# Attention's values as one product of blocks: seven block products in place of eight

## The chip, the cores and the metric

The kernel runs on one core of one Trainium2 chip. The core has five engines that run their own instruction streams and wait for each other on semaphores: TensorE (PE in the profile; its weight loads are PEld), VectorE (DVE), ScalarE (ACT), GpSimd (POOL), and SyncE (SP), which here issues nearly all of the loads. The metric is the device time of one execution in microseconds. The kernel before takes 977.26 us, the median of three runs (977.25 to 977.32). A difference of under 0.2% (about 2 us) can't be told from no change here.

## What is computed

Two layers on 512 frames of 1024 channels, all in float32. Layer 0 mixes frames by pooling, layer 1 by attention; each is followed by a gated MLP with a short convolution. The change is in layer 1, in the product that makes the attention's values. Cut to that part:

```python
h = rmsnorm(x, mix_norm[1])            # 512 frames x 1024 channels
qkv = h @ w_qkv                        # 1024 -> 3 * 1024
q, k, v = jnp.split(qkv, 3, axis=-1)
q = head_rmsnorm(q.reshape(B, S, N_HEADS, HEAD_DIM), q_norm)
k = head_rmsnorm(k.reshape(B, S, N_HEADS, HEAD_DIM), k_norm)
v = v.reshape(B, S, N_HEADS, HEAD_DIM)
...
p = jax.nn.softmax(s, axis=-1).astype(vb.dtype)
return jnp.einsum('bhqk,bkhd->bqhd', p, vb)
```

The values are thus the product of a 512 x 1024 matrix of frames and a 1024 x 1024 matrix of weights.

## The kernel before, in words

The residual stream lies in eight tiles `X[k]` of 128 channels x 512 frames. A product in full precision is made of three fast products: every operand is split into a high part (a rounded copy, made by ScalarE) and a low part (the rest, made by a subtraction on VectorE), and `mm3` (L117) sends three matmuls to TensorE: high x high, high x low, low x high (L119, L120, L121). `split` (L93) makes the two parts (L98 on ScalarE, L99 on VectorE), `split_scaled` (L101) the same with a factor per partition (L103, L104), and `load_split` (L106) loads a tile of weights of 128 x 1024 into one of three raw buffers (DMA at L113) and splits it into one of two pairs of buffers, `wh` and `wl`.

`ffn` (L377) is the gated MLP. Most of its hidden tiles are made by `strassen` (L532), which already spends seven block products where eight would be plain; the differences of its weight blocks are VectorE's (L537 to L540). Its last group of output products (`out`, adds to `X` at L608) is the work just ahead of the attention.

`attention` (L641) first makes `XS`, the scaled stream split in high and low parts (16 tiles, in `set2`). Then, in this order of the code: `project(0)` (L671), the queries and keys of the first four heads; `late`, which holds the squares of these, their sums (L681) and the norms made from them (L697); `values(0)` and `values(1)` (L707), the two halves of 512 value channels; between these `channel_major` (L750) twice, the transposes of the first heads' queries and keys (L756). Each of `project` and `values` goes through `products` (L658): four weight tiles of 128 x 1024 (two groups of 128 input channels each), and for each group four tiles of 128 frames, so 8 x 4 x 3 = 96 matmuls of 512 columns into four PSUM banks. A half's four results are divided among the tiles `set1`, as `V`, by 16 calls of `split_scaled` on 128 x 128 pieces, with the factor `rcol` of each frame.

Then comes the loop over 16 heads and four tiles of 128 frames (`scores`, `turn`, `mix`: scores, their transposes, the mix of the values), with the rest of the projections and the output product as fill. `scores` reads the bias of its head from one of two tiles `BT`, which SyncE loads from memory (L781). Before the first scores, 44 matmuls of `project(1)` run as fill; its weights' low parts are made by GpSimd, not by VectorE.

What sets the order: in the loop over the heads and in `ffn`, TensorE's order is written out by hand (`manual_schedule`). The part that the change touches, `project(0)` to `values(1)`, has no order written out for any engine: a planner in the framework orders each engine's instructions when the kernel is built. The memory comes from pools with a lifetime: `ffn(0)` has the pool `b0`, the attention `ba` in the same place after it, the second `ffn` `b1`. PSUM has eight banks, under three names: four called S, two P, two Q.

Of the kernel before, what the change touches and what calls it, by code (L numbers as in the profile page):

```python
# [68 lines left out]
def trunk(ctx: ExitStack, tc: tile.TileContext, xt, xT, cols, band, edge, poolw, gv, wout, wqk, wv, wo, rel, out):  # L69
# [15 lines left out]
    def psum(tag, name, bufs=2):  # L85
        return ps.tile([P, S], F32, name=name, tag=tag, bufs=bufs)
# [6 lines left out]
    def split(raw, hi, lo, eng=None, eng_hi=None):  # L93

        if eng_hi:
            eng_hi.tensor_copy(hi, raw)
        else:
            nc.scalar.activation(hi, raw, AF.Copy)  # L98
        return (eng or nc.vector).tensor_sub(lo, raw, hi.bitcast(F32))  # L99
# [17 lines left out]
    def mm3(o, sh, sl, mh, ml, first, last):  # L117

        yield nc.tensor.matmul(o, sh, mh, start=first, stop=False)  # L119
        yield nc.tensor.matmul(o, sh, ml, start=False, stop=False)  # L120
        yield nc.tensor.matmul(o, sl, mh, start=False, stop=last)  # L121

    def run(steps):
        step = None
        for step in steps:
            pass
        return step
# [513 lines left out]
    def attention():  # L641
# [2 lines left out]
        O2 = {}  # L644


        PT = [[big.tile([P, 4 * (TT - 1) + 1, P], F32R, name=f"pt{b}{c}") for c in "hl"] for b in range(2)]

        KL = [[big.tile([P, S], F32R, name=f"kl{b}{e}") for e in range(2)] for b in range(2)]
        for b in range(2):  # L650
            for e in range(2):
                nc.gpsimd.memset(KL[b][e][(1 - e) * HD:(2 - e) * HD].bitcast(F32), 0.0)
        BT = [big.tile([P, S], F32, name=f"B{b}") for b in range(2)]
        for b in range(2):
            nc.gpsimd.memset(BT[b][:HD, :HD], -NEG)
        V = {}

        def products(ov, w, name, eng=None, evict=None):  # L658

            for kk in range(4):  # L660
                hi, lo = load_split(w[kk], 1024, f"{name}_{kk}", eng=eng)

                for c, t in [(c, t) for c in range(2) for t in range(TT)] if kk < 3 else [(c, t) for t in range(TT) for c in range(2)]:
                    k = 2 * kk + c
                    s = slice(c * S, (c + 1) * S)
                    q = slice(t * P, (t + 1) * P)
                    yield from mm3(ov[t], XS[k][:, q], XS[KD + k][:, q], hi[:, s], lo[:, s], k == 0, k == KD - 1)
                    if kk == 3 and c and evict:
                        evict(t)
# [34 lines left out]

            late.append(norms)

        def values(half, banks):  # L707
            ov = [psum(banks[t // 2], f"v{half}_{t}", BANKS[banks]) for t in range(TT)]

            def evict(t):  # L710
                for hh in range(2):
                    V[t, 2 * half + hh] = vt = set1[(t * 2 + half) * 2 + hh].rearrange("p (h a d) -> p h a d", h=4, a=2)
                    v4 = ov[t][:, hh * 256:(hh + 1) * 256].rearrange("p (h d) -> p h d", d=HD)
# [4 lines left out]
            yield from products(ov, wv[half], f"wv{half}", evict=evict)  # L718

        def output(ps_, after=None):  # L720

# [51 lines left out]
        def scores(h, t):  # L773

            p, e = divmod(h, 2)
            q, k, kl = QK[p, 0][e], QK[p, 1][e], KL[p % 2][e]
            if t == 0:

                base = rdram[h, :]
                for r, n in ((0, S - HD), (HD, S)):  # L780
                    nc.sync.dma_start(BT[h % 2][r:r + HD, S - n:], bass.AP(tensor=base.tensor, offset=base.offset + HD, ap=[[1, HD], [1, n]]))  # L781
            n = (t + 1) * P
            nw = max(n, 256)

            sc = psum("S", f"sc{h}_{t}", 4)
            nc.tensor.matmul(sc[:, :nw], q[:, t * P:n], k[:, :nw], start=True, stop=False)
            nc.tensor.matmul(sc[:, :nw], q[:, t * P:n], kl[:, :nw], start=False, stop=True)
            SM[h, t] = s_ = big.tile([P, n], F32, name=f"sb{h}_{t}", tag=f"sb{t}")
# [16 lines left out]
        def mix(h):  # L805

            p, e = divmod(h, 2)
            hs = slice(e * HD, (e + 1) * HD)
            oo = psum("S", f"oo{h}", 4)
            if p not in O2:  # L810
                O2[p] = big.tile([P, S], F32, name=f"o2_{p}", tag="o2", bufs=4)
# [25 lines left out]
        with tc.manual_schedule(engines={mybir.EngineType.PE}):  # L837
# [37 lines left out]
                    kept += 1  # L875
            fill(nb + FO)
        assert kept == NPAIR
        return lambda after: output((6, 7), after)

    def last_pairs(rest, c, name):  # L880
# [90 lines left out]
```

## Time and profile before

| what | value |
|---|---|
| median of three runs | 977.26 us |
| span of the profiled execution | 975.1 us |
| left around the span, against the median | 2.16 us |
| TensorE busy | 967.0 us (99%) |
| VectorE busy | 807.8 us (83%) |
| ScalarE busy | 541.4 us (56%) |
| GpSimd busy | 103.2 us (11%) |
| granted TensorE clock | 1.000 |

The profiled execution's time is its span and what lies around it; the profile states the span alone, so 2.16 us is taken as constant. The attention's part that matters here goes from 380 us, where the last output product of the first `ffn` ends, to 454.7 us, where the first scores start. The profile is read in stages: the whole-run shares in the table say which engine is busiest on average, and a row over a stretch says which one is short of time there. A row of the timeline gives the start, the duration, the engine, the line, the operation, and in brackets the idle time before it and what ended that.

### The profile page before, as it was taken

The page shows a single profiled execution, that of the slowest core. Times are in us where ns is not written, and L with a number is a line of the kernel's source. Part 1 is how long each engine was busy: PE and PEld are TensorE (multiplying, and loading weights), DVE is VectorE, ACT ScalarE, POOL GpSimd, SP SyncE. Part 2 cuts the span into 40 slices and gives each one's busy share as a digit, 9 for nine tenths or more (in the row PEclk, how much of TensorE's full clock was granted, in tenths as well). Part 3 has the DMA queues.
Part 4 walks back from the last instruction along what each step waited for, and adds up shares of the span by engine and source line. Part 5 has one row for each costly group of instructions (what it writes and reads, how often), then busy time and mean ns, then how long its engine had stood idle before and what let it go on. Part 6 is the DMA issues. An engine that isn't in the chain of part 4 may idle for free.

```text
span 975.1 us, 15058 instructions
## 1 busy us (share of the span) xinstructions
PE 967.0 (99%) x5582; PEld 847.0 (87%) x5582; DVE 807.8 (83%) x1468; ACT 541.4 (56%) x926; POOL 103.2 (11%) x90
## 2 busy tenths in 40 slices
PE   9999999999999999999999999999999999999998
PEld 8788999998899888888888787888999989899986
DVE  8999989999999854442777887999989998999953
ACT  7665454544454544345898988656545444455421
POOL 2300000000000013204534442000000000000000
PEclk9999999999999999999999999999999999999999
DMA  9222323333333234232333341232333333233323
GB/s 341 70 85 71 117 89 111 119 113 98 104 92 103 68 90 150 89 119 96 112 114 105 96 118 54 87 110 79 104 110 118 92 105 111 86 117 98 100 71 111
DMA packets 37433, 102.91 MB, mean 106 GB/s; under 512 B 4432, under 2 KB 7904, under 8 KB 37360
## 3 DMA queue, kind: packets, MB, share of 16 engines
q1 hardware_dynamic: 37296, 101.90, 33.7%
q8 instruction: 44, 0.72, 0.3%
q14 instruction: 29, 0.24, 0.1%
q0 software_dynamic: 32, 0.04, 0.0%
q10 hardware_dynamic: 32, 0.00, 0.0%
HBM read 95.60 MB, written 2.14 MB: 100 GB/s over the span
## 4 chain that ended last, share of the span: by engine, by line
PE 94%; DVE 4%; ACT 2%; issue 0%; DMA 0%; DVEq 0%; ACTq 0%
PE out L120 8%; PE out L119 8%; PE out L121 8%; PE st_t L120 5%; PE st_t L119 5%; PE st_t L121 5%; PE st_b L120 4%; PE st_b L119 4%; PE st_b L121 4%; PE st_t L555 4%; PE gv L120 4%; PE gv L119 4%; PE gv L121 4%; PE qk L120 3%; PE qk L119 3%; PE qk L121 3%
## 5 line engine op out<-in xcount | busy, mean ns | idle before, releaser
L98 ACT ACTIVATE g_h<-gv_r 128x1024 fp32r<-128x1024 f32 x68 | 57.7, 848 | 79.2 <-PE st_t L120 37.5
L120 PE MATMUL out<-one,ow_h 128*128 128x512 f32 x224 | 88.1, 393 | 0.0
L119 PE MATMUL out<-one,ow_h 128*128 128x512 f32 x224 | 87.8, 392 | 0.0
L121 PE MATMUL out<-one,ow_l 128*128 128x512 f32 x224 | 87.7, 392 | 0.0
L98 ACT ACTIVATE ow_h<-wo_r 128x640 fp32r<-128x640 f32 (+1 forms) x64 | 50.5, 789 | 59.6 <-PE out L120 47.0
L608 DVE TENSOR_TENSOR X<-out,X 128x512 f32<-128x512 f32 (+1 forms) x65 | 43.9, 677 | 38.1 <-PE out L121 37.8
L98 ACT ACTIVATE g_h<-sa 128x1024 fp32r<-128x1024 f32 x34 | 36.1, 1060 | 59.1 <-PE st_t L120 42.4
L99 DVE TENSOR_TENSOR g_l<-gv_r,g_h 128x1024 fp32r<-128x1024 f32 x68 | 64.6, 950 | 4.8 <-ACT g_h L98 4.5
L99 DVE TENSOR_TENSOR ow_l<-wo_r,ow_h 128x640 fp32r<-128x640 f32 (+1 forms) x64 | 56.5, 882 | 0.0
L419 DVE SCALAR_TENSOR_TENSOR c<-a,col,c 128x511 f32<-128x511 f32 (+1 forms) x76 | 56.2, 742 | 0.1
L120 PE MATMUL st_t<-h,g_h 128*128 128x256 f32 x192 | 54.3, 283 | 0.0
L119 PE MATMUL st_t<-h,g_h 128*128 128x256 f32 x192 | 54.3, 283 | 0.0
L121 PE MATMUL st_t<-h,g_l 128*128 128x256 f32 x192 | 54.3, 283 | 0.0
L121 PE MATMUL st_t<-two,g_l 128*128 128x256 f32 x192 | 54.0, 281 | 0.0
L120 PE MATMUL st_t<-two,g_h 128*128 128x256 f32 x192 | 53.9, 281 | 0.0
L119 PE MATMUL st_t<-two,g_h 128*128 128x256 f32 x192 | 53.8, 280 | 0.0
L121 PE MATMUL qk<-wqk_h,two 128*128 128x512 f32 x128 | 51.4, 402 | 0.0
L119 PE MATMUL qk<-wqk_h,two 128*128 128x512 f32 x128 | 50.8, 409 | 0.0
L120 PE MATMUL qk<-wqk_l,two 128*128 128x512 f32 x128 | 50.8, 397 | 0.0
L121 PEld LDWEIGHTS out<-one,ow_l 128*128 128x128 f32 x224 | 42.3, 189 | 6.6
L119 PEld LDWEIGHTS out<-one,ow_h 128*128 128x128 f32 x224 | 42.4, 189 | 5.9
L120 PEld LDWEIGHTS out<-one,ow_h 128*128 128x128 f32 x224 | 42.5, 190 | 5.3 <-DVE one L99 0.2
(331 smaller groups left out, 3154.3 us busy)
## 6 DMA issues: line engine op xcount, KB each, us to landing
gv_r<-gv SPq DMA_DIRECT2D x86, 512.0 KB, 3.6
wo_r<-wout SPq DMA_DIRECT2D x32, 384.0 KB, 3.1
wo_r<-wout SPq DMA_DIRECT2D x32, 320.0 KB, 2.9
wqk_r<-wqk SPq DMA_DIRECT2D x16, 512.0 KB, 3.5
wv_r<-wv SPq DMA_DIRECT2D x8, 512.0 KB, 3.5
wo_r<-wo SPq DMA_DIRECT2D x8, 512.0 KB, 3.5
xt<-xt SPq DMA_DIRECT2D x4, 512.0 KB, 5.2
X<-xT SPq DMA_DIRECT2D x8, 256.0 KB, 7.5
```

What stands on the lines that cost most here:

```text
L98: nc.scalar.activation(hi, raw, AF.Copy)
L99: return (eng or nc.vector).tensor_sub(lo, raw, hi.bitcast(F32))
L119: yield nc.tensor.matmul(o, sh, mh, start=first, stop=False)
L120: yield nc.tensor.matmul(o, sh, ml, start=False, stop=False)
L121: yield nc.tensor.matmul(o, sl, mh, start=False, stop=last)
L419: nc.vector.scalar_tensor_tensor(c[:, j:], a[:, :S - j], cw[2 - j], c[:, j:], op0=OP.mult, op1=OP.add)
L555: nc.tensor.matmul(o, hi[:, c], B[i, name], start=i == 0, stop=False)
L608: nc.vector.tensor_add(X[d][:, fs], o[:, fs], X[d][:, fs])
```

## The change

The frames are cut in two halves of 256 and the input channels in two halves of 512: a11, a21 (the first 512 channels of the two frame halves), a12, a22 (the last 512). The weights are cut in b11, b12, b21, b22 (input half, output half). Four sums of frame blocks and four of weight blocks, and seven block products in place of eight, give the same result. Each block product is 2 weight tiles x 2 channel groups x 2 frame tiles x 3 = 24 matmuls of 512 columns, so 168 in all, where the two halves had 192.

- `token_sums` makes the frame sums s1 to s4 from scaled copies of `X` (8 copies by ScalarE, 8 sums by VectorE) and splits each (8 high parts by ScalarE, 8 low parts by VectorE) into the 16 tiles of `set1`, which later take the values.
- `value_pair` loads the eight raw weight tiles into a pool `pre` of eight buffers, and VectorE makes the weight differences in place (8 subtractions of 128 x 1024). Each of the seven products splits its own two weight tiles; for one product the raw block was overwritten and is loaded again (two more loads). Three products are chained in the two S banks without clearing them, two in the two Q banks; ScalarE copies the partial sums out three times two, VectorE adds three times two, and the values are divided from SBUF copies or from PSUM.
- `channel_major` for the first heads stands behind the fifth product.
- The tiles `PT`, `BT`, the scores' and the output tiles move to a pool `heads`, opened when `pre` has been closed, in the same place in memory.

```diff
+        def token_sums(pre):
...
+            for kk in range(2):
+                ya, yb = (pre.tile([P, 2, S], F32, name=f"y{c}{kk}", tag="pre", bufs=8) for c in "ab")
+                for y, k0 in ((ya, 2 * kk), (yb, 2 * kk + 4)):
+                    for c in range(2):
+                        nc.scalar.activation(y[:, c], X[k0 + c], AF.Copy, scale=col[:, C_MIXN[1] + k0 + c:C_MIXN[1] + k0 + c + 1])
...
+                nc.vector.tensor_add(s1, a21, a22)
+                nc.vector.tensor_sub(s2, s1, a11)
+                nc.vector.tensor_sub(s3, a11, a21)
+                nc.vector.tensor_sub(s4, a12, s2)
+                for n, x in (("s2", s2), ("s3", s3), ("s1", s1), ("s4", s4)):
+                    split(x, *(f.rearrange("p (c n) -> p c n", c=2) for f in form[n][kk]))
...
+        def value_pair(pre, form):
...
+            b = [[raw(kk // 2, 2 * (kk % 2) + j, f"vb{kk}_{j}") for kk in (0, 2, 3, 1)] for j in range(2)]
...
+            def parts(x, name):
+                hi, lo = (wp.tile([P, 1024], F32R, name=f"{name}_{c}", tag=f"w{c}", bufs=2) for c in "hl")
+                split(x, hi, lo)
+                return hi, lo
...
+            A, B, C = bank("S", "va"), bank("P", "vb"), bank("Q", "vc")
+            x1, copy = copies(A, "x1")
+            product("a11", A, lambda j: parts(b[j][0], f"wv1_{j}"), True, copy)
+            for j in range(2):
+                b11, b12, b22, b21 = b[j]
+                nc.vector.tensor_sub(b11, b12, b11)
+                nc.vector.tensor_sub(b12, b22, b12)
+                nc.vector.tensor_sub(b22, b22, b11)
+            product("a12", B, lambda j: parts(b[j][3], f"wv2_{j}"), True, add(x1, B))
+            for j in range(2):
+                nc.vector.tensor_sub(b[j][3], b[j][3], b[j][2])
+            y6, copy = copies(A, "y6")
+            product("s2", A, lambda j: parts(b[j][2], f"wv6_{j}"), False, copy)
+            for i in range(2):
+                store(x1[i], i, 0)
+            product("s3", C, lambda j: parts(b[j][1], f"wv7_{j}"), True, nothing)
+            y5, copy = copies(A, "y5")
+            product("s1", A, lambda j: parts(b[j][0], f"wv5_{j}"), False, copy)
+            for i in range(2):
+                add(y5, C)(i)
+            yield
+            for i in range(2):
+                store(y5[i], 2 + i, 1)
...
+            product("s4", A, b22, False, nothing)
+            for i in range(2):
+                store(A[i], i, 1)
+            product("a22", C, lambda j: parts(b[j][3], f"wv4_{j}"), False, add(y6, C))
+            for i in range(2):
+                store(y6[i], 2 + i, 0)
...
-        run(project(0, "SS"))
-        while late:
-            late.pop(0)()
-        run(values(0, "PQ"))
-        for i in range(2):
-            channel_major(0, i)
-        run(values(1, "SS"))
+        with tc.tile_pool(name="pre", bufs=1) as pre:
+            run(project(0, "SS"))
+            form = token_sums(pre)
+            while late:
+                late.pop(0)()
+            pair = value_pair(pre, form)
+            next(pair)
+            for i in range(2):
+                channel_major(0, i)
+            run(pair)
+        closing = ExitStack()
+        heads = closing.enter_context(tc.tile_pool(name="bh", bufs=1))
```

More of the change, by code (lines that the diff above doesn't have):

```diff
@@ L115, in load_split, with mm3 @@
         return hi, lo
[L117 to L121, printed above, removed]
+    def mm3(o, sh, sl, mh, ml, first, last, **how):
+        yield nc.tensor.matmul(o, sh, mh, start=first, stop=False, **how)
+        yield nc.tensor.matmul(o, sh, ml, start=False, stop=False, **how)
+        yield nc.tensor.matmul(o, sl, mh, start=False, stop=last, **how)
     def run(steps):
@@ L705, in project @@
             late.append(norms)
-        def values(half, banks):
-            ov = [psum(banks[t // 2], f"v{half}_{t}", BANKS[banks]) for t in range(TT)]
-            def evict(t):
+        def token_sums(pre):
+            form = {}
+            for z, n in enumerate(("s2", "s3", "s1", "s4")):
+                js = ((0, 1, 4, 5), (10, 11, 14, 15), (8, 9, 12, 13), (2, 3, 6, 7))[z]
+                form[n] = [[set1[js[2 * c + kk]] for c in range(2)] for kk in range(2)]
+            for kk in range(2):
[3 more added lines that the diff above has]
+                        nc.scalar.activation(y[:, c], X[k0 + c], AF.Copy, scale=col[:, C_MIXN[1] + k0 + c:C_MIXN[1] + k0 + c + 1])
+                s1, s2, s3, s4 = (w[:, z * S:(z + 1) * S].rearrange("p (c n) -> p c n", c=2)
+                                  for w in (pre.tile([P, 2 * S], F32, name=f"s{c}{kk}", tag="pre", bufs=8) for c in "ab") for z in range(2))
+                (a11, a21), (a12, a22) = ((y[:, :, :HALF], y[:, :, HALF:]) for y in (ya, yb))
+                nc.vector.tensor_add(s1, a21, a22)
[4 more added lines that the diff above has]
+                    split(x, *(f.rearrange("p (c n) -> p c n", c=2) for f in form[n][kk]))
+            return form
@@ new lines, in value_pair, with raw, stationary, product @@
+        def value_pair(pre, form):
+            def raw(half, kk, name):
+                w = pre.tile([P, 2 * S], F32, name=name, tag="pre", bufs=8)
+                nc.sync.dma_start(w, wv[half, kk])
+                return w
+            b = [[raw(kk // 2, 2 * (kk % 2) + j, f"vb{kk}_{j}") for kk in (0, 2, 3, 1)] for j in range(2)]
+            def stationary(n, k, i):
+                if n in form:
+                    return [x[:, k % 2 * HALF + i * P:k % 2 * HALF + (i + 1) * P] for x in form[n][k // 2]]
+                kb, t = {"a11": (0, 0), "a12": (4, 0), "a22": (4, 2)}[n]
+                q = slice((t + i) * P, (t + i + 1) * P)
+                return XS[kb + k][:, q], XS[KD + kb + k][:, q]
+            def product(n, o, weight, first, after):
+                for j in range(2):
+                    hi, lo = weight(j)
+                    for c, i in [(c, i) for c in range(2) for i in range(2)] if not j else [(c, i) for i in range(2) for c in range(2)]:
+                        s = slice(c * S, (c + 1) * S)
+                        run(mm3(o[i], *stationary(n, 2 * j + c, i), hi[:, s], lo[:, s], first and j == 0 and c == 0, j == 1 and c == 1,
+                                skip_group_check=not first))
+                        if j and c:
+                            after(i)
+            def parts(x, name):
+                hi, lo = (wp.tile([P, 1024], F32R, name=f"{name}_{c}", tag=f"w{c}", bufs=2) for c in "hl")
+                split(x, hi, lo)
+                return hi, lo
+            def bank(tag, name):
+                return [psum(tag, f"{name}{i}", BANKS[tag * 2] if tag == "S" else 2) for i in range(2)]
+            def copies(o, name):
+                x = [pre.tile([P, S], F32, name=f"{name}{i}", tag="vx", bufs=4) for i in range(2)]
+                return x, lambda i: nc.scalar.activation(x[i], o[i], AF.Copy)
+            def store(x, t, half):
@@ new lines, in nothing @@
+            def nothing(i):
+                pass
+            A, B, C = bank("S", "va"), bank("P", "vb"), bank("Q", "vc")
[7 more added lines that the diff above has]
+            product("a12", B, lambda j: parts(b[j][3], f"wv2_{j}"), True, add(x1, B))
@@ new lines, in value_pair @@
+            for j in range(2):
+                nc.vector.tensor_sub(b[j][3], b[j][3], b[j][2])
[8 more added lines that the diff above has]
+                add(y5, C)(i)
@@ L810, in mix @@
             if p not in O2:
-                O2[p] = big.tile([P, S], F32, name=f"o2_{p}", tag="o2", bufs=4)
+                O2[p] = heads.tile([P, S], F32, name=f"o2_{p}", tag="o2", bufs=4)
             for c in range(2):
@@ L823, in attention @@
         rcol, r2, late = None, small("r2", TT), []
-        run(project(0, "SS"))
-        while late:
-            late.pop(0)()
-        run(values(0, "PQ"))
-        for i in range(2):
-            channel_major(0, i)
-        run(values(1, "SS"))
+        with tc.tile_pool(name="pre", bufs=1) as pre:
[10 more added lines that the diff above has]
+        heads = closing.enter_context(tc.tile_pool(name="bh", bufs=1))
+        PT = [[heads.tile([P, 4 * (TT - 1) + 1, P], F32R, name=f"pt{b}{c}") for c in "hl"] for b in range(2)]
+        BT = [heads.tile([P, S], F32, name=f"B{b}") for b in range(2)]
+        for b in range(2):
+            nc.gpsimd.memset(BT[b][:HD, :HD], -NEG)
         tiles_ = [(h, t) for h in range(H) for t in range(TT)]
```

14 lines of the change are left out of this document (7 added, 7 removed).

## Prediction

> **What bounds the kernel now.** I read the page first (busy shares, then the chain that ended last), then the stretches around the change, then TensorE's timeline in them, then who waits for memory. From the page:
>
> ```profile
> span 975.1 us, 15058 instructions
> ...
> PE 967.0 (99%) x5582; PEld 847.0 (87%) x5582; DVE 807.8 (83%) x1468; ACT 541.4 (56%) x926; POOL 103.2 (11%) x90
> ...
> PE 94%; DVE 4%; ACT 2%; issue 0%; DMA 0%; DVEq 0%; ACTq 0%
> ```
>
> TensorE bounds the whole run: 94% of the last chain. So a matmul removed is its issue time saved, unless TensorE then waits. The next engine, VectorE, is at 83% on average, and this change takes work from TensorE and gives work to VectorE. Hence the stage matters. The stretches (columns: length, then busy us and instructions of PE, PEld, DVE, ACT, POOL, then clock, DMA share, GB/s), cut at the end of the first `ffn`, the start of the values, the end of two eighths of them, and their end:
>
> ```profile
> 380.00:398.60 18.60, 18.60 (x84) 15.40 (x83) 7.01 (x8) 6.87 (x10) 3.52 (x7) 1.00 0.36 110
> 398.60:411.00 12.40, 12.40 (x60) 10.40 (x59) 6.24 (x17) 4.33 (x9) 5.11 (x4) 1.00 0.26 88
> 411.00:444.50 33.50, 33.44 (x151) 27.10 (x150) 15.41 (x31) 14.78 (x33) 4.02 (x3) 1.00 0.33 97
> ```
>
> TensorE is full in all three, VectorE under half busy. There is room, but it is finite: 31.0 - 7.01 - 6.24 = 17.7 us in the first two stretches.
>
> **The change part by part.** *The matmuls.* TensorE's timeline in the values (start, duration; equal neighbours are merged, with their count):
>
> ```profile
> 398.58 1.07 PE L119 MATMUL v<-wv_h,two 128*128 128x512 f32 x4
> ...
> 400.18 0.95 PE L150 MATMUL n_st<-ones,n_acc 128*128 128x1 f32 x8
> 400.99 0.47 PE L121 MATMUL v<-wv_h,two 128*128 128x512 f32 x1
> ...
> 421.71 0.71 PE L756 MATMUL zt<-ident,z 128*128 128x128 f32 x5
> 422.17 0.48 PE L119 MATMUL v<-wv_h,two 128*128 128x512 f32 x1
> ...
> 431.12 0.39 PE L119 MATMUL v<-wv_h,two 128*128 128x512 f32 x1
> ...
> 433.17 1.20 PE L119 MATMUL v<-wv_h,two 128*128 128x512 f32 x4
> 434.43 0.50 PE L120 MATMUL v<-wv_l,two 128*128 128x512 f32 x1
> ...
> 444.53 0.39 PE L119 MATMUL qk<-wqk_h,two 128*128 128x512 f32 x1
> ```
>
> From 431.12 to 433.17 nine matmuls start, 0.228 us apart (each lasts 0.39, but they overlap). 192 - 168 = 24 fewer save 24 x 0.228 = 5.5 us. [...]
>
> The values take 444.53 - 398.58 = 45.95 us. 192 x 0.228 = 43.8, the statistic's eight small matmuls 0.8 (400.18 to 400.99) and eight transposes at (422.17 - 421.71) / 5 = 0.09, 0.7, make 45.3. The remaining 0.6 are waits of the old order, one seen at 433.17: four matmuls of 0.228 should end at 434.08, and the next starts at 434.43. The new order has its own waits, so these 0.6 go.
>
> *When the new work may start.* The frame sums lie in the new pool `pre`, which opens where `b0` lay.
>
> ```profile
> SPq L781 <- PE out L121: 5.6, 1, 5.6
> ```
>
> ```profile
> 380.05 2.21 POOL L652 MEMSET kl<- 64x512 f32 x4 [2.07 <-PE out L121]
> ```
>
> ```profile
> 379.97 0.69 DVE L608 TENSOR_TENSOR X<-out,X 128x512 f32<-128x512 f32 x1 [3.16 <-PE out L121]
> ```
>
> The bias loads (5.6 us) and GpSimd's memset, which write fresh tiles of `ba`, both wait for the last output matmul and go at 380. I read that as: no tile of a later pool is written before the earlier pool is done. Half of the frame sums also need the last `X`, done at 380.66. So nothing new starts before 380.
>
> *VectorE's queue up to the third product.* Prices: a group of whole tiles, and three neighbours that run back to back.
>
> ```profile
> L99 DVE TENSOR_TENSOR wv_l<-wv_r,wv_h 128x1024 fp32r<-128x1024 f32 x8 | 9.8, 1225 | 19.1 <-ACT wv_h L98 18.9
> ```
>
> ```profile
> 240.91 0.68 DVE L537 TENSOR_TENSOR sa<-gv_r 128x512 f32<-128x512 f32 x1
> 241.51 0.69 DVE L539 TENSOR_TENSOR sb<-gv_r,gv_r 128x512 f32<-128x512 f32 x1
> 242.12 0.68 DVE L594 TENSOR_TENSOR c<-v,c 128x512 f32<-128x512 f32 x1
> ```
>
> Back to back a 512-wide operation costs 0.60, 0.08 less than it lasts, so a 1024-wide one 1.225 - 0.08 = 1.14. Work for VectorE between 380 and the first low part of the third product (s2), the first to need the differences: the old work of the two stretches, 7.01 + 6.24 = 13.2, which holds three low parts of value weights; 8 frame sums and 8 low parts of them, 16 x 0.60 = 9.6; eight weight differences, 8 x 1.14 = 9.1 (two products' code stands behind six of them, the third's behind all eight); five low parts in place of three, 2.3. In all 34.2 us. TensorE arrives there two products after 398.58, 48 x 0.228 + 0.8 = 11.7, at 410.3, and can send one matmul ahead for each of its two banks: 410.8. That leaves 30.8 us. So TensorE waits 34.2 - 30.8 = 3.4 us if VectorE is never idle, in the second product or the third. VectorE also waits for ScalarE, which must first copy the frames, four 512-wide copies for each half of the sums, and hand over each high part. So VectorE's idle time lies between nothing and those eight copies, 4.8 at 0.60 each (VectorE's 512-wide price, the nearest row), of which its old work covers a part; I take two thirds, 3.1. The wait is then 6.5; its ends are 0 (if everything that can be late is put late: six frame low parts 3.6, four differences 4.6, which is more than 3.4) and 8.2. I stay near the top because the order is not made for this: the code lists the differences ahead of the low parts they delay, and in the rows above two sums of weights for a coming tile (L537, L539) run ahead of the older L594. The eight transposes (0.7) can run inside the wait: net 5.8.
>
> *The pair of weight buffers.* A tile now feeds 12 matmuls, 2.7 us, not 24.
>
> ```profile
> 432.05 1.06 ACT L98 ACTIVATE wv_h<-wv_r 128x1024 fp32r<-128x1024 f32 x1 [3.67 <-PE v L121]
> ```
>
> ```profile
> 433.15 2.58 DVE L99 TENSOR_TENSOR wv_l<-wv_r,wv_h 128x1024 fp32r<-128x1024 f32 x2 [4.38 <-ACT wv_h L98]
> ```
>
> ```profile
> 442.12 2.98 ACT L103 ACTIVATE one<-v,n_y 128x128 fp32r<-128x128 f32 x9 [0.42 <-DVE one L104]
> ```
>
> A pair is free at 432.05 - 0.24 (the next tile's first matmul, 431.12 + 3 x 0.228 = 431.81), and the first matmul on the new low part goes at 434.43: 2.62 later, less 0.46 for two matmuls sent ahead is 2.16, against 2.73. So 0.57 are to spare. One foreign 1.14 in front costs 0.6; eight pieces of values at 2.98 / 9 = 0.33, all in front, cost 2.0. Such groups stand beside three products (x1, y5, A), the copies and sums of the partial results with them: 0 to 6 us. I take 0.6 each, 1.8, since the pieces alternate between two engines and leave gaps.
>
> *The hand-over to `project(1)`.*
>
> ```profile
> 439.29 1.06 ACT L98 ACTIVATE wqk_h<-wqk_r 128x1024 fp32r<-128x1024 f32 x1 [4.82 <-PE v L121]
> ```
>
> ```profile
> 440.49 2.39 POOL L99 TENSOR_TENSOR wqk_l<-wqk_r,wqk_h 128x1024 fp32r<-128x1024 f32 x1 [14.66 <-ACT wqk_h L98]
> ```
>
> Its first pair took 442.88 - 439.29 = 3.6, and 0.24 for the release, under 5.5 us of matmuls; now 2.7 cover it, and one matmul, 0.2: 3.8 - 2.9 = 0.9, between 0 and 0.9.
>
> *At nothing:* ten weight loads in place of eight, and all bias loads behind the whole of `pre` on SyncE's queue, where `wqk` loads stand behind them. The 44 matmuls of fill (44 x 0.228 = 10.0) cover the last sums and pieces (2 x 0.60 + 8 x 0.33 = 3.8), the memset and the bias load.
>
> ```profile
> B<-rdram SPq DMA_DIRECT2D x4, 128.0 KB, 3.0
> ```
>
> ```profile
> 454.73 0.28 PE L786 MATMUL sc<-zh,zh 128*128 128x256 f32 x1
> ```
>
> With its 3.0 that is 7 to 8 of 10 us ahead of the first scores (454.73 before); if the values' tail takes 3 longer, each further us is one of the scores'. The six partial copies are ScalarE's, beside matmuls.
>
> *Sum* on the profiled execution: -5.5 - 0.6 + 5.8 + 1.8 + 0.9 = +2.4; span 977.5, and with the same 2.16 around it **979.7 us** (0.25% slower). Behind 454 TensorE is bound by its own order, so the shift stays.
>
> **The rivals.** *Faster: VectorE's queue serves TensorE first* (0.22). If what isn't urgent is put behind the second and third products' low parts, the wait of 5.8 is gone, and later waits of some 2 remain: -5.5 - 0.6 + 2 = -4.1, **973.2**. For it: 17.7 us of room, and the planner did keep 45.3 of 45.95 full. Against: 16 + 8 + 14 new operations. It decides at 410.8: is the first low part of s2 there?
>
> *Faster or the same: the frame sums start early* (0.10). If `pre` is free by about 370, four `X` are final and half of the 9.6 is done ahead: 5.8 falls to 1.0, **974.9**. Against it stand both rows at 380.
>
> *Slower: the clock drops in the wait* (0.12). In the values TensorE is busy for 33.44 of 33.50 us, and the clock reads 1.00 in every stretch above. A wait of 6 us in one piece would be new to this trace; if matmuls behind it ran at half rate for one to two weight tiles, 12 to 24 would take 0.228 more each, 2.7 to 5.5: 979.7 + 3.4 = **983.1**. That half rate is my supposition, not a row. [...]
>
> **How the numbers follow.** The forecast has 0.50; its own range, with the wait from 3.4 to 7.2 after the transposes, the pairs from 0.8 to 3 and the hand-over from 0.4, is 975.8 to 982.3, of which 0.32 lie above 979.2 and 0.18 within. The faster rival gives 0.19 faster and 0.03 same; early sums 0.07 and 0.03; the clock 0.12 slower; the rest (0.06) is split 0.02, 0.02, 0.02. Together: faster 0.28, same 0.26, slower 0.46. Under 0.2% (1.95 us) isn't told from no change. Range: 973.2 to 983.1, from one rival's value to the other's.
>
> **What would show it.** Right: the values' matmuls (168) from about 398.6 to 447; one TensorE wait of 4 to 7 us between 404 and 418 with VectorE busy over 90% from 396 to 416, and six differences ahead of the second product's low part; smaller waits of about 0.6 later; first scores near 457. Wrong: VectorE idle for over 3 us in that stretch while TensorE waits (then ScalarE or a load is late); frame sums before 380; a clock under 1.00; or values that end before 442, which would make the first rival right.

## The result, and the profile after

| | before | after |
|---|---|---|
| median | 977.28 us (17 runs, 976.97 to 978.00) | 979.06 us (17 runs, 978.77 to 979.84) |
| ratio | | 1.0019, 95% interval 1.0012 to 1.0026 |
| profiled execution: time, span | | 978.88, 977.1 us |

The change makes the kernel slower by 1.8 us, the size of the smallest difference that can be told here. The forecast was 979.7. Around the span of this profiled execution lie 978.88 - 977.1 = 1.8 us, not the 2.16 that were taken as constant. From the page of the kernel after, the lines that stand against those of before:

```profile
span 977.1 us, 15095 instructions
...
PE 964.2 (99%) x5558; PEld 841.5 (86%) x5558; DVE 838.1 (86%) x1504; ACT 558.8 (57%) x954; POOL 104.4 (11%) x90
...
PE 90%; DVE 5%; ACT 2%; issue 1%; DMA 1%; POOL 1%; SPq 0%; DVEq 0%; POOLq 0%; ACTq 0%
```

TensorE has 24 instructions and 2.8 us of busy time less, yet its share of the last chain falls from 94% to 90%. What it gave up went to others: VectorE has 5% where it had 4%, and issue, a load and GpSimd, at nothing before, have 1% each. The stretches, cut as before, show where (columns as in the prediction):

```profile
380.00:398.60 18.60, 18.60 (x83) 15.22 (x82) 16.40 (x23) 15.09 (x25) 3.94 (x5) 1.00 0.52 192
398.60:411.00 12.40, 10.97 (x50) 8.27 (x49) 12.40 (x17) 7.31 (x12) 0.00 (x0) 1.00 0.34 137
411.00:444.50 33.50, 30.88 (x134) 23.70 (x133) 27.19 (x50) 20.53 (x42) 7.92 (x7) 1.00 0.14 48
```

In the middle row VectorE is busy for 12.40 of 12.40 us, and TensorE, which was full there, for 10.97. The clock column stays at 1.00. Now TensorE's timeline of the values, the rows around its waits, and 413.56, the first matmul on a low part of the third product:

```profile
398.96 0.95 PE L150 MATMUL n_st<-ones,n_acc 128*128 128x1 f32 x8
399.77 0.47 PE L119 MATMUL va<-wv_h,two 128*128 128x512 f32 x1
...
403.93 0.73 PE L119 MATMUL vb<-wv_h,two 128*128 128x512 f32 x2 [0.69 <-ACT wv_h L98]
...
407.22 0.50 PE L120 MATMUL vb<-wv_l,two 128*128 128x512 f32 x1 [0.27 <-DVE wv_l L99]
...
410.70 0.50 PE L120 MATMUL vb<-wv_l,two 128*128 128x512 f32 x1 [0.47 <-DVE wv_l L99]
...
413.56 0.39 PE L120 MATMUL va<-wv_l,one 128*128 128x512 f32 x1
...
417.49 0.73 PE L119 MATMUL vc<-wv_h,one 128*128 128x512 f32 x2 [1.05 <-ACT wv_h L98]
418.06 0.39 PE L120 MATMUL va<-wv_l,one 128*128 128x512 f32 x1
...
423.92 0.73 PE L119 MATMUL va<-wv_h,one 128*128 128x512 f32 x2 [0.42 <-ACT wv_h L98]
424.87 0.44 PE L849 MATMUL zt<-ident,z 128*128 128x128 f32 x2 [0.22 <-POOL z L698]
...
437.09 0.50 PE L120 MATMUL va<-wv_l,one 128*128 128x512 f32 x1 [0.70 <-DVE wv_l L99]
...
440.33 0.50 PE L120 MATMUL vc<-wv_l,two 128*128 128x512 f32 x1 [0.22 <-DVE wv_l L99]
...
445.46 0.39 PE L119 MATMUL qk<-wqk_h,two 128*128 128x512 f32 x1
446.70 0.50 PE L120 MATMUL qk<-wqk_l,two 128*128 128x512 f32 x1 [0.85 <-POOL wqk_l L99]
```

The waits are many and short. The brackets understate them, since they count from the modelled end of the matmul ahead; counting matmuls is safer. The row at 418.06 is the 65th matmul since 399.77 (ahead of it two products, 48, the third product's first tile, 12, and four matmuls sent ahead on high halves): 64 x 0.228 = 14.6 us, and it starts 18.3 us later, so **3.7 us are lost up to there**. From 418.06 to 445.46 are 27.4 us, for 104 matmuls (23.7) and eight transposes (0.7): **3.0 more are lost**. The stage from the statistic to the first matmul of `project(1)` is 445.46 - 398.96 = 46.5 us, 0.55 more than before. From there to the first scores it was 454.73 - 444.53 = 10.2 us, and is now 11.35 (the first scores matmul starts at 456.81): 1.15 more, at the hand-over. The stage begins 0.4 later (398.96 after 398.58); 0.25 of that is there already at the last output matmul of the first `ffn` (379.80 after 379.55), ahead of all that was changed. Behind the first scores all is as before (520.3 us to the end of the span, 520.4 before). 0.4 + 0.55 + 1.15 - 0.1 is the 2.0 that the span grew.

Why VectorE is the one that is late at 418 is in its own timeline of the kernel after:

```profile
382.89 0.69 DVE L717 TENSOR_TENSOR sa<-ya,yb 128x512 f32<-128x512 f32 x1 [1.97 <-ACT yb L713]
...
404.82 1.22 DVE L786 TENSOR_TENSOR vb<-vb,vb 128x1024 f32<-128x1024 f32 x1
405.95 1.22 DVE L99 TENSOR_TENSOR wv_l<-vb,wv_h 128x1024 fp32r<-128x1024 f32 x1
407.09 1.22 DVE L784 TENSOR_TENSOR vb<-vb,vb 128x1024 f32<-128x1024 f32 x1
...
411.78 1.22 DVE L99 TENSOR_TENSOR wv_l<-vb,wv_h 128x1024 fp32r<-128x1024 f32 x1
412.91 1.21 DVE L786 TENSOR_TENSOR vb<-vb,vb 128x1024 f32<-128x1024 f32 x1
...
414.12 1.27 DVE L774 TENSOR_TENSOR x<-x,vb 128x512 f32<-128x512 f32 x2
415.32 1.22 DVE L789 TENSOR_TENSOR vb<-vb,vb 128x1024 f32<-128x1024 f32 x1
...
416.56 1.22 DVE L99 TENSOR_TENSOR wv_l<-vb,wv_h 128x1024 fp32r<-128x1024 f32 x1
```

From the second row on there is no bracket: VectorE never idles. The last row makes the low part that TensorE takes at 418.06. Ahead of it stand a difference that it needs (412.91), two sums of partial results that it doesn't (414.12), and a difference that only the seventh product needs (L789, 415.32).

### The profile page after: what moved, and what is told of

It reads as the page before. It is cut to its first block, busy times and chain, and to the rows that moved or that the text cites. A ratio compares the mean times of both kernels' runs of the same rounds, so it can differ in the third digit from the quotient of the medians.

```text
span 977.1 us, 15095 instructions
## 1 busy us (share of the span) xinstructions
PE 964.2 (99%) x5558; PEld 841.5 (86%) x5558; DVE 838.1 (86%) x1504; ACT 558.8 (57%) x954; POOL 104.4 (11%) x90
## 4 chain that ended last, share of the span: by engine, by line
PE 90%; DVE 5%; ACT 2%; issue 1%; DMA 1%; POOL 1%; SPq 0%; DVEq 0%; POOLq 0%; ACTq 0%
PE out L120 8%; PE out L119 8%; PE out L121 8%; PE st_t L120 5%; PE st_t L119 5%; PE st_t L121 5%; PE st_b L120 4%; PE st_b L119 4%; PE st_b L121 4%; PE st_t L555 4%; PE gv L120 4%; PE gv L121 4%; PE gv L119 4%; PE qk L120 3%; PE qk L119 3%; PE qk L121 3%
## 5 line engine op out<-in xcount | busy, mean ns | idle before, releaser
L119 PEld LDWEIGHTS out<-one,ow_h 128*128 128x128 f32 x224 | 42.4, 189 | 5.9
L883 DVE CUSTOM_DVE_ANT_0 sb<-sc,B 128x128 f32<-128x128 f32 (+1 forms) x64 | 31.0, 485 | 18.8 <-PE sc L880 18.1
```

What stands on the lines that cost most here:

```text
L119: yield nc.tensor.matmul(o, sh, mh, start=first, stop=False, **how)
```

## The experiments

The theory: up to 418 TensorE waits for VectorE's queue. The rivals: the two pairs of weight buffers, ScalarE's high parts, the hand-over. One table first. "Stretch" runs from the last output matmul of the first `ffn` to the first scores matmul and holds everything that the change touches; "outside" is the rest of the span of the same profiled execution.

| kernel | median us (runs) | ratio to before, 95% | stretch | outside |
|---|---|---|---|---|
| before | 977.28 (17) | | 75.2 | 899.9 |
| after | 979.06 (17) | 1.0012 to 1.0026 | 77.0 | 900.1 |
| e1, no differences | 973.86 (5) | 0.9953 to 0.9978 | 72.0 | 899.9 |
| e2, third high buffer | 976.60 (11) | 0.9985 to 1.0003 | 74.3 | 900.1 |
| e3, differences on GpSimd | 990.98 (4) | 1.0124 to 1.0152 | 90.2 | 900.4 |
| e4, before less 24 matmuls | 973.38 (5) | 0.9945 to 0.9970 | 70.9 | 900.7 |
| e5, last difference late | 982.77 (5) | 1.0041 to 1.0067 | 76.7 | 903.0 |
| e6, hand-over | 977.86 (11) | 0.9997 to 1.0014 | 75.9 | 900.2 |
| e7, three together | 977.12 (11) | 0.9988 to 1.0006 | 72.8 | 902.6 |
| e8, and z copies on ScalarE | 977.09 (11) | 0.9987 to 1.0005 | | |
| e9, e5 with the zero elsewhere | 978.80 (11) | 1.0015 to 1.0033 | 76.7 | 900.2 |
| e10, e7 with the zero elsewhere | 974.25 (7) | 0.9959 to 0.9981 | 72.3 | 900.2 |
| e11, after and a small tile | 981.69 (5) | 1.0032 to 1.0060 | 77.2 | 902.7 |
| e12, buffer and hand-over | 976.62 (11) | 0.9984 to 1.0002 | 74.8 | 900.0 |

**e1: the eight weight differences left out.**

```diff
             for j in range(2):
                 b11, b12, b22, b21 = b[j]
-                nc.vector.tensor_sub(b11, b12, b11)
-                nc.vector.tensor_sub(b12, b22, b12)
-                nc.vector.tensor_sub(b22, b22, b11)
+                pass
...
-                nc.vector.tensor_sub(b[j][3], b[j][3], b[j][2])
+                pass
```

> The changed kernel without its eight weight differences on VectorE (the products then use the blocks as loaded; this part of the computation is left out). Up to the first low part of the third product's second weight tile (418.06) TensorE has lost 3.7 us: that matmul is the 65th since 399.77, 64 x 0.228 = 14.6, and it starts 18.3 later. Theory, VectorE's queue: all of these 3.7 stand behind whole differences of 1.14 us, eight of them, 9.1, so at least 3 of 3.7 go, and the run is near 975.7 (975.2 to 976.2). Rival, the two pairs of weight buffers: a pair is free only when its 12 matmuls are done, whatever VectorE does, so the waits at the hand-overs stay, and at most 1 us goes: 978.1 or more. Rival, ScalarE late with the high parts (its rows end the waits at 403.93, 417.49, 423.92): those three stay, 1 to 1.5 us go, near 977.7.

Measured 973.86, 5.2 less than after. TensorE's first matmul of the values, the one at 414.60 on the low part in question, the two waits that its timeline marks in the values, and the first matmul of `project(1)`:

```profile
399.69 0.47 PE L119 MATMUL va<-wv_h,two 128*128 128x512 f32 x1
...
414.60 0.48 PE L120 MATMUL va<-wv_l,one 128*128 128x512 f32 x1
...
423.75 0.50 PE L120 MATMUL va<-wv_l,one 128*128 128x512 f32 x1 [0.28 <-DVE wv_l L99]
...
435.25 0.50 PE L120 MATMUL vc<-wv_l,two 128*128 128x512 f32 x1 [0.27 <-DVE wv_l L99]
...
440.37 0.39 PE L119 MATMUL qk<-wqk_h,two 128*128 128x512 f32 x1
```

The low part taken at 418.06 is taken at 414.60, 14.9 us after the first product's start in place of 18.3: 3.4 of the 3.7 are gone, with pairs and ScalarE as they were. The theory holds, and it was too modest (975.7): the values take 40.7 from first matmul to `project(1)` where they took 45.7, 1.7 lost in all where it was 6.7. So some 1.6 us of what is lost behind 418 hangs on VectorE's queue too.

**e2: a third buffer for the high half.**

```diff
+            ring = iter("wwp" * 5)
+
             def parts(x, name):
-                hi, lo = (wp.tile([P, 1024], F32R, name=f"{name}_{c}", tag=f"w{c}", bufs=2) for c in "hl")
+                lo = wp.tile([P, 1024], F32R, name=f"{name}_l", tag="wl", bufs=2)
+                if next(ring) == "w":
+                    hi = wp.tile([P, 1024], F32R, name=f"{name}_h", tag="wh", bufs=2)
+                else:
+                    hi = pre.tile([P, 1024], F32R, name=f"{name}_h", tag="ph", bufs=1)
                 split(x, hi, lo)
                 return hi, lo
...
-                return load_split(wv[1, 2 + j], 1024, f"wv3_{j}")
+                raw = wp.tile([P, 1024], F32, name=f"wv3_{j}_r", tag="wr")
+                nc.sync.dma_start(raw, wv[1, 2 + j])
+                return parts(raw, f"wv3_{j}")
```

> The changed kernel with a third buffer for the high half of a weight tile, so that ScalarE's copy (1.06) no longer waits for the release of the tile two before; the low half still has two. Theory, VectorE's queue: the low parts come as late as before, nothing moves up to 418: between 978.5 and 979.1, the small waits behind 420 a little shorter. Rival, the two pairs: the turnaround 2.16 falls by ScalarE's 1.06, and the waits at the hand-overs behind 420 (0.42, 0.70, 0.22 and what stands with them, 2.9 us in all from 418 to 445) and part of the earlier ones go: 977.0 or less.

Measured 976.60, 2.5 less than after: the rival's time. But the theory is right up to 418, and the rival only behind it:

```profile
413.10 0.50 PE L120 MATMUL va<-wv_l,one 128*128 128x512 f32 x1 [0.74 <-DVE wv_l L99]
...
418.14 0.50 PE L120 MATMUL va<-wv_l,one 128*128 128x512 f32 x1 [1.20 <-DVE wv_l L99]
...
443.31 0.39 PE L119 MATMUL qk<-wqk_h,two 128*128 128x512 f32 x1
443.98 0.50 PE L120 MATMUL qk<-wqk_l,two 128*128 128x512 f32 x1 [0.28 <-POOL wqk_l L99]
```

418.14 where it was 418.06: ahead of it the buffer gains nothing. From there to `project(1)` it is 25.2 us in place of 27.4: 2.2 of the 3.0 lost there are gone, and another 0.6 at the hand-over, whose wait is shorter here (11.35 to the first scores became 10.8). The high halves are there early now, and no bracket names ScalarE any more, yet the low part of 418 is waited for as long: so VectorE was the binding one there, though the row at 417.49 of the kernel after names ScalarE.

**e3: the differences on GpSimd.**

```diff
-                nc.vector.tensor_sub(b11, b12, b11)
+                nc.gpsimd.tensor_sub(b11, b12, b11)
```

The same for the other two lines in the loop and for the last difference.

> The changed kernel with the eight weight differences on GpSimd in place of VectorE, at 2.39 us each by its row for a 1024-wide difference (the low part of project(1)'s weights), 19.1 in all. Theory, VectorE's queue: the waits of 3.7 up to 418 shrink as without the differences, as long as GpSimd is in time: its first three from 398 to 405, the next three from 405 (after the low part of the first product's second tile) to 412.4, the third product's second tile is wanted at about 413: 976 to 977. Rival, GpSimd becomes the late one: each of its six differences comes 1.25 us later than VectorE's would, the third and fourth products wait for them 2 to 3 us: 978.5 to 980.

Measured 990.98, 12 more than after: neither. GpSimd's timeline, then VectorE's, of the same stretch:

```profile
404.23 2.40 POOL L784 TENSOR_TENSOR vb<-vb,vb 128x1024 f32<-128x1024 f32 x1 [1.16 <-DVE wv_l L99]
406.58 2.36 POOL L786 TENSOR_TENSOR vb<-vb,vb 128x1024 f32<-128x1024 f32 x1
408.89 2.35 POOL L785 TENSOR_TENSOR vb<-vb,vb 128x1024 f32<-128x1024 f32 x1
```

```profile
404.67 1.98 DVE L133 SCALAR_TENSOR_TENSOR n_t<-n_y 128x4 f32<-128x4 f32 x1
406.68 2.27 DVE L134 TENSOR_TENSOR n_t<-n_t,n_a 128x4 f32<-128x4 f32 x1
408.98 2.27 DVE L135 SCALAR_TENSOR_TENSOR n_y<-n_t,n_y 128x4 f32<-128x4 f32 x1
```

Three operations on four columns, which take 0.15 us each in the kernel after, last 2 us, and each ends within 0.02 us of the end of a GpSimd difference (404.23 + 2.40 = 406.63 and 404.67 + 1.98 = 406.65). VectorE stands still here while GpSimd works, so a difference moved there took 2.0 to 2.3 us from VectorE in place of 1.14. The three read two operands from SBUF (L133 the same tile twice), as the differences do. Operations with one were not held up: VectorE's copy at 399.54 takes 0.69 and its two reductions at 400.15 take 1.27, beside the GpSimd differences of 398.19 and 400.66; in the kernel after they take 0.68 and 1.26. Nor were L774's two sums at 420.32, with one operand in PSUM (1.27 beside L698, 1.27 in the kernel after). The low part behind these rows comes late, and then, in TensorE's timeline and the stretches of e3 (cut at 407.0, 412.8, 417.0; last but two columns: clock):

```profile
412.86 0.80 PE L120 MATMUL vb<-wv_l,two 128*128 128x512 f32 x1 [5.65 <-DVE wv_l L99]
```

```profile
407.00:412.80 5.80, 0.21 (x1) 0.00 (x0) 5.70 (x6) 0.00 (x0) 4.23 (x2) 0.76 0.00 0
412.80:417.00 4.20, 4.14 (x10) 3.27 (x11) 2.37 (x7) 1.78 (x4) 2.38 (x1) 0.51 0.00 2
```

After 5.65 us without work the granted clock is 0.51 for 4.2 us, and ten matmuls start where eighteen would at 0.228. It falls in the middle of that wait: the 5.80 us from 407.0 read 0.76, and if they are 1.00 up to the fall and 0.51 behind it, then it comes, as an estimate, some 2.8 us after TensorE stopped at 407.2. It falls a second time at about 427.1. The two matmuls that start there take 1.18 us, the two ahead of them 0.73, and from 432.51 to 436.78 each lasts 0.63, as at 0.51 behind the first wait, where most last 0.39 at 1.00. The whole stretch from 411.0 to 444.5 reads 0.76. Ahead of this second fall TensorE had waited in one piece only for 2.19 us:

```profile
426.10 0.73 PE L119 MATMUL va<-wv_h,one 128*128 128x512 f32 x2 [2.19 <-ACT wv_h L98]
427.05 1.18 PE L119 MATMUL vc<-wv_h,one 128*128 128x512 f32 x2 [0.21 <-ACT wv_h L98]
431.92 0.79 PE L120 MATMUL va<-wv_l,one 128*128 128x512 f32 x1 [3.69 <-DVE wv_l L99]
432.51 0.63 PE L121 MATMUL va<-wv_h,one 128*128 128x512 f32 x1
...
436.78 0.63 PE L121 MATMUL vc<-wv_h,one 128*128 128x512 f32 x1
437.21 0.47 PE L120 MATMUL vc<-wv_l,one 128*128 128x512 f32 x1
437.51 0.39 PE L121 MATMUL vc<-wv_h,one 128*128 128x512 f32 x1
```

This is the mechanism of the rival "the clock drops in the wait", seen, half rate included, but at waits that the change itself doesn't make: the kernel after waits at most 1.05 us in one piece in the values, at a clock of 1.00.

**e4: the kernel before without the 24 matmuls of one weight tile of the second half.** The weight tile is the third of the second half's four, two groups of 128 channels.

```diff
+                    if name == "wv1" and kk == 2:
+                        continue
                     yield from mm3(ov[t], XS[k][:, q], XS[KD + k][:, q], hi[:, s], lo[:, s], k == 0, k == KD - 1)
```

> The kernel before with the 24 matmuls of one of the second half's channel groups left out (loads, splits and all else stay; the sums lack that group). It prices the removed matmuls by themselves: 24 x 0.228 = 5.5, 971.8. Rival: part of it is given back at once, because the weight tiles behind it have 24 matmuls less to be made ready under, 972.5 to 974.

Measured 973.38: 3.9 less, not 5.5, where the rival has it. TensorE, and the ScalarE rows that it waits for:

```profile
435.19 1.20 PE L119 MATMUL v<-wv_h,two 128*128 128x512 f32 x4 [1.20 <-ACT wv_h L98]
```

```profile
432.72 1.06 ACT L98 ACTIVATE wv_h<-wv_r 128x1024 fp32r<-128x1024 f32 x1 [3.67 <-PE v L121]
434.08 1.06 ACT L98 ACTIVATE wv_h<-wv_r 128x1024 fp32r<-128x1024 f32 x1 [0.30 <-PE v L121]
```

The second of these high halves can be copied only when an older tile's pair is free, and the 24 matmuls that hid its copy and split are the ones that are gone. In the table the stretch is 4.3 shorter (70.9 after 75.2): 1.2 of 5.5 us are given back at once, about this one wait, even with nothing put in their place. The profiled execution also is 0.8 longer outside (900.7 after 899.9), where nothing was changed; why is open.

**e5 and e9: the last difference held back.** A zero, written by ScalarE from the third product's copy, is added in the difference, so that it can't run earlier, whatever order the planner picks.

```diff
-            for j in range(2):
-                nc.vector.tensor_sub(b[j][3], b[j][3], b[j][2])
...
+            zero = small("zero", 1)
+            nc.scalar.activation(zero, y6[1][:, :1], AF.Copy, scale=0.0)
+            for j in range(2):
+                nc.vector.scalar_tensor_tensor(b[j][3], b[j][3], zero, b[j][2], op0=OP.add, op1=OP.subtract)
```

> The changed kernel with the two differences that only the last product needs (L789) held back behind the third product, by a zero that ScalarE writes from that product's copy and that the difference adds; nothing else is changed. VectorE's queue ahead of 418.06 is 2 x 1.14 = 2.3 us shorter. Theory, VectorE's load sets the 3.7 lost up to there: about 2.3 of them go, and the waits behind stay, 976.8 (976.3 to 977.4). Rival, the pairs of buffers take over at once: each tile freed later by what VectorE gained, so no more than 1 us goes, 978.0 or more.

Measured 982.77, 3.7 more than after, against both. The table says where for the profiled execution, which took 981.47 at a mean clock of 1.000: the stretch is 0.3 shorter, and outside, where not one instruction was changed, are 2.9 us more. The other four executions took 982.76 to 983.13 at a mean clock of 0.997 or 0.998; none of them was profiled. e9 has the zero in the pool `pre`:

```diff
-            zero = small("zero", 1)
+            zero = pre.tile([P, 1], F32, name="zero")
```

> The held-back last difference once more, with the zero's 4 bytes per partition in the pool pre (which closes with the values) and not in tmp, from which on all later tiles of the whole program had moved; the order of the instructions is the same. In the first form the values' stage itself was 0.28 shorter (first va matmul to first qk matmul 45.41 after 45.69), but TensorE came to the stage 1.4 later (last output matmul 381.16 after 379.80) and needed 1.5 more behind the first scores (521.8 after 520.3). Theory, the tile's place costs these 2.8: they vanish, and 978.8 (978.3 to 979.3) is left, so that holding back the difference gains almost nothing. Rival, the longer run is the order's own doing: 982 to 983 again.

Measured 978.80 in the median, as the tile's place predicts. But the eleven executions fall into two groups: six took 978.52 to 978.80 at a mean clock of 1.000, five 979.91 to 981.18 at 0.998. A mean clock lower by 0.002 over 977 us is, as an estimate, one piece of some 4 us at e3's half of the clock (0.002 x 977 / 0.5). None of the five was profiled; the profiled one (978.71) reads 1.00 all through the values, with a longest wait of 1.37. So the difference held back by itself is worth 0.3 us in the median, not 2.3, and in five of eleven executions it costs about 1.3. The low part of 418.06 is there 16.5 us after the first product's start in place of 18.3, as it should be; the gain is lost again behind it. VectorE, GpSimd and TensorE of e9:

```profile
422.62 4.04 DVE L795 SCALAR_TENSOR_TENSOR vb<-vb,zero,vb 128x1024 f32<-128x1024 f32 x2
```

```profile
420.57 6.99 POOL L698 TENSOR_TENSOR z<-z,qk_y 128x512 f32<-128x512 f32 x4 [34.45 <-DVE qk_y L696]
```

```profile
427.62 0.44 PE L851 MATMUL zt<-ident,z 128*128 128x128 f32 x2 [1.37 <-POOL z L698]
428.70 0.50 PE L120 MATMUL va<-wv_l,one 128*128 128x512 f32 x1 [0.64 <-DVE wv_l L99]
```

The two differences now run beside the norms' products on GpSimd (L698), and take 4.04 us where the same two take 2.48 in e10, which has them ahead of L698. It is e3's standstill again. In the kernel after, L698 stands at 421.70, since the small operations that lead to it are late in VectorE's full queue; in the kernel before (L703 there) it stood at 405.29, beside a single low part, and took 5.11.

**e6: VectorE makes the first low part of `project(1)`.**

```diff
-                hi, lo = load_split(w[kk], 1024, f"{name}_{kk}", eng=eng)
+                hi, lo = load_split(w[kk], 1024, f"{name}_{kk}", eng=None if name == "wqk1" and kk == 0 else eng)
```

> The changed kernel with the low part of project(1)'s first weight tile on VectorE (1.14) in place of GpSimd (2.39). Theory, the hand-over: the wait of TensorE at 446.70 (it starts 1.24 after the first matmul of project(1) where 0.46 would be its turn) falls to nothing, 0.8 to 1.0 less, 978.1 to 978.3. Rival: VectorE is full of the last pieces from 445.1 to 447.5, the low part queues behind them and comes no earlier, 978.8 to 979.3.

Measured 977.86, 1.2 less than after, a little more than the theory's 0.8 to 1.0. The values take the 45.7 us that they took; the first matmul of `project(1)` to the first scores takes 10.2 us, as before the change, in place of 11.35. The hand-over is worth its 1.15.

**e7 and e8: together.** e7 has the edits of e2, e5 and e6; e8 besides copies all of `project(0)`'s results on ScalarE (`if t % 2` becomes `if t % 2 and c`).

> The third buffer for the high half, the held-back last difference and VectorE's hand-over together, the output complete. The third buffer alone took 2.4 (to 976.6). Theory, two independent stretches, VectorE's queue up to 418 and the pairs behind it: another 2.3 for the difference, and little more for the hand-over, whose wait was already 0.2 there: 974.3 (973.8 to 975.0), 0.3% under the kernel before. Rival, the stretches are one chain and what is gained ahead of 418 is waited for behind it: 976.0 to 976.6.

> The run with the three together, and besides project(0)'s two z copies of VectorE (0.68 each, 0.60 back to back, at 397.7 and 400.0) on ScalarE. Theory, VectorE's queue: 1.2 us less ahead of 418, of which 1.4 are still lost there: 973.2 to 973.6. Rival, ScalarE then is late with the high parts of the first two products (0.60 each for the copies ahead of them): no gain, 974.3 or a little more.

Measured 977.12 and 977.09. e7 is outside both, 0.5 above its rival's range, and not for the rival's reason: its stretch is 4.2 us shorter than that of after, and outside it loses 2.5. e8 gains nothing over e7, as its rival had it, though 2.8 above the rival's 974.3, which was counted from the time that was expected of e7; of e8 only its time is used, so that why is open.

**e10: e7 with the zero in `pre`; e11: the kernel after with the small tile alone.**

> The run with the three together (third high buffer, held-back difference, hand-over), with the zero in the pool pre. Theory, the tile's place: its last output matmul at 380.89 and 521.7 behind the first scores come back to 379.8 and 520.3, so 977.1 becomes 974.6 (974.0 to 975.2), 0.3% under the kernel before. Rival, the order's own doing: 976.8 to 977.4.

> The changed kernel as it is, with nothing added but the one-column tile in tmp and ScalarE's write of it (0.19 us, read by nobody). Theory, the tile's place: some 2.8 more, 981.8 (981 to 982.6), all of it outside the values, half ahead of 380 and half behind 457. Rival: 979.0 to 979.4, and what lengthened the two runs was the new order.

Measured 974.25 and 981.69: both as the tile's place predicts. e10 is the fastest complete version, 0.9970 of before (0.9959 to 0.9981) and 4.8 us below after. The values of e11 take 45.8 us, as in the kernel after (45.7); what is longer are matmuls elsewhere. A group of the first `ffn`'s output products between 300 and 380 us, of after and then of e11 (busy us, mean ns):

```profile
L119 PE MATMUL out<-one,ow_h 128*128 128x512 f32 x52 | 20.3, 390 | 0.0
```

```profile
L119 PE MATMUL out<-one,ow_h 128*128 128x512 f32 x51 | 20.1, 395 | 0.0
```

**e12: the third buffer and the hand-over, without the held-back difference.**

> The third high buffer and VectorE's hand-over, the last difference where the change has it. It splits the gain of the three together (974.25) from the third buffer alone (976.60). Theory, VectorE's 2.3 us count only once the pairs no longer wait behind them: the hand-over gives what is left of its wait in the run with the third buffer (0.67 between the first two matmuls of project(1), 0.23 would be their turn, 0.4 to 0.6 in all), 976.1 (975.7 to 976.4), and the held-back difference is worth 1.5 to 2.1 here, where alone it was worth 0.3. Rival: the hand-over is worth its full 1.2 here too, 975.4, and the difference 1.1.

Measured 976.62, above both (976.1 and 975.4): the hand-over adds nothing to the third buffer in the median, and the held-back difference is worth 976.62 - 974.25 = 2.4 here, about the whole 2.3 that its two operations cost. The profile of e12 shows where the hand-over's gain went. From `project(1)` to the first scores it is 10.2 us (10.8 in e2), but ScalarE's copy of the first product's second tile waits for its load:

```profile
397.75 1.06 ACT L98 ACTIVATE wv_h<-vb 128x1024 fp32r<-128x1024 f32 x1 [1.51 <-DMA vb<-wv]
```

In e2 the same row waits 0.40, at 396.73. With a third buffer this copy is free to stand ahead of others, and depends on a load that lands within a microsecond of the time it is wanted. In e7 it waits 1.51 and in e10 1.18: all three profiles with both edits have the longer wait. The loads are issued at the same time in e2 and e12 (six from 388.09 and from 388.02), and land later in e12 (6.3 us in the median, 5.5 in e2); why is open.

## Why the prediction was right, and where not

The forecast was 0.25% slower; it is 0.19%. By its own steps:

- **The matmuls (-5.5) and the old waits (-0.6).** Right as a count: the values issue 168 matmuls at 0.228. But the matmuls saved are not time saved by themselves: in the old order e4 gets 4.3 in its stretch for 24 of them, for what they covered has to be covered otherwise. The prediction has that loss in its step on the buffers, not in this one.
- **Nothing before 380.** Right: the frame sums start at 382.89 in the kernel after. No early sums.
- **VectorE's queue (+5.8).** The cause was right (e1), its size and shape were not. The sum had 37.3 us of VectorE from 380 to the first low part of the third product, 34.2 of work and 3.1 of idle time (two thirds of 4.8 are 3.2), and so a wait of 6.5. Measured, that low part (411.78) is made by 412.9, after 32.9 us: 30.7 of work and 2.2 of idle time, 1.97 of it in one wait for ScalarE's copies of the frames (382.89). By the count TensorE would take it 50 matmuls, 11.4 us, after 399.77, at 411.2; it takes it at 413.56, 2.4 late. Two terms of the sum were too large, and they are the step that failed. The work, by 3.5: only six of the eight differences stand ahead of this low part (2.3), and old work, the norms' small operations for one, came behind it (the other 1.2, not broken down). And the idle time, by 0.9. The two other differences, at 412.91 and 415.32, then delay the second tile's low part, and 3.7 are lost there; that the sum with VectorE never idle gave 3.4 is chance. The wait in one piece of 4 to 7 us was wrong as well, and so was its reason, six differences ahead of the second product's low part: the row at 405.95 has three differences ahead of it, then they alternate. The planner doesn't follow the code's order, so the same lateness comes in pieces of up to 1.05 us. That also decided the rival with the clock: it reads 1.00 beside these pieces, and 0.51 behind one wait of 5.65 (e3).
- **The pair of buffers (+1.8).** The mechanism was right (e2), the size too small: of 3.0 lost behind 418 the third high buffer alone takes back 2.2. (Without the differences 1.6 of the same 3.0 go, so that the two causes overlap.) What the step left out is that the three store groups aren't the only foreign work: the norms, pushed back by VectorE's queue, bring GpSimd's L698 to 421.70, in the middle of the low parts (two of them take 3.37 there, where two back to back take 2.36 in e10 at 415.40). No step of the prediction had that; what it costs TensorE was not measured by itself.
- **The hand-over (+0.9).** Right: 1.15, and e6 gets 1.2 back.
- **The sum.** 5.8 + 1.8 = 7.6 against 6.7 measured, 0.9 against 1.15, and 0.4 by which the stage began later, which no step has: +2.4 against +2.0 in the span. Two errors of opposite sign, one too large by 2, one too small by 1, leave a sum that is right to 0.4; that is luck in part. With 1.8 around the span in place of 2.16 the forecast would have been 979.3.
- **The rivals.** "VectorE's queue serves TensorE first" is not this kernel: the low part that it asks for at 410.8 is taken at 413.56. e10, which puts two differences behind the third product and takes off the other two limits besides, comes near it (974.25 for its 973.2). The frame sums did not start early (382.89), and the clock did not fall (1.00 in every stretch). Where it fell, in e3, the half rate that this rival supposed is what was read, 0.51, for ten matmuls behind the wait of 5.65, where the rival counted 12 to 24.

## What to carry to other kernels

When matmuls are exchanged for vector work, don't price the matmuls alone: every weight tile then has less work to hide the next tile's copy, split and release under, and that gives back a part before the new work costs anything (1.2 of 5.5 in e4's stretch). Count the new work against the time at which the first product needs it, not against the average share of the engine. And mend the limits together: the held-back difference is worth 0.3 us alone in the median and 2.4 once the buffers no longer wait behind it.

## What the runs showed of the hardware

- **A tile of one column in the wrong pool costs more than the whole change.** e11 adds a tile of 4 bytes per partition (four buffers) to `tmp`, from which on the later pools lie elsewhere. A group of the first `ffn`'s output matmuls goes from 390 to 395 ns, and the run is 2.6 us longer, 0.1 of it in the values. That the place of the operands is the cause is shown by e9 and e10, which have the same order as e5 and e7 and only the tile elsewhere (981.47 became 978.71 in the profiled executions, 977.13 became 974.25); what about the place slows these matmuls is open.
- **GpSimd and VectorE held each other up** in operations with two SBUF operands: on VectorE 0.15 us became 2.27 (e3) and 2.48 became 4.04 (e9), on GpSimd the 5.11 of L698's four in the kernel before became 6.99 (e9). VectorE's copy and reductions, with one operand, kept their time beside GpSimd (0.69 and 1.27 in e3). GpSimd's 11% share is no free capacity for such operations.
- **The clock halved around longer waits of TensorE**, in e3 twice: some 2.8 us (an estimate from the mean of 0.76) into one of 5.65, and about 1.0 us after the end of one of 2.19. Once TensorE worked again it read 0.51 for 4.2 us after the first; after the second, matmuls started 0.43 us apart in place of 0.228 for 5.3 us. It read 1.00 around waits of up to 1.05 (the kernel after), 1.37 (e9) and 1.75 (e12). Where the limit lies these runs don't show.
